# A threshold search by counting: the third count of each round moved from VectorE to ScalarE

## The chip, the cores and the metric

The kernel runs on one core of one Trainium2 chip. Its time is the device time of one execution in microseconds, the median of several runs. The core's engines are named as in the profile: PE is TensorE (PEld its weight loads), ACT is ScalarE, DVE is VectorE, POOL is GpSimd and SP is SyncE, which here only issues DMAs. Each engine runs its own instructions in order.

## The reference

One inference step of a decoder layer, for a prompt of 1024 tokens and for a sample of 8 sequences with 4 new tokens each over a paged past of 8192. Sparse attention and retention run side by side:

```python
hp = _rmsnorm(xp, g_pre[i])
qa, ka, va, qi, ki, wi, ga, qb, kb, vb, gb = _project(hp, w_in[i], pos_p)
oa = _dsa_prompt(qa, ka, va, qi, ki, wi, rel_bias)          # top-256 keys by an indexer, then attention
ob, sp = _retention(qb, kb, vb, zeros)                       # 8 heads, chunks of 128
xp = _merge(xp, oa, ob, ga, gb, p_prompt[i], w_out[i], g_post[i], w_ple_up[i], w_ple_gate[i])
...
oa = _dsa_sample(qa, ka, va, qi, ki, wi, cache_k[i], cache_v[i], cache_kidx[i], page_table, rel_bias)
ob, ss = _retention(qb, kb, vb, state_ret[i])
```

The change lies in the selection of the sample's keys. In the reference this is

```python
score = jnp.einsum('bqh,bqhs->bqs', wi, jax.nn.relu(s))     # 32 queries, 8196 keys each
score = jnp.where(valid, score, -jnp.inf)
top_val, top_idx = lax.top_k(score, topk)                   # topk = 256
```

The kernel does not sort. For each of the 32 queries it looks for the threshold that 256 scores reach, and then selects by comparison.

## The kernel before, in words

The order of the work is: norms, projections and index scores (the signs of the search start at 317.6 us, the first projection of head pair 0 at 297); retention over four pairs of heads, `hp` 0 to 3; attention of the prompt, with the sample's attention threaded through it; output projection and gate.

The threshold search of the sample, `bisect_sample`, runs beside the retention. The 32 queries' scores lie on 128 partitions: partition 32·i + q holds a quarter i of query q's keys, in 2048 + 32 columns (`NX`). `u16` holds the upper 16 bits of each score, turned so that they order as unsigned numbers. `search` finds in eight rounds the 16-bit threshold of each query, two bits a round: with a step `s` that is divided by four each round, three thresholds are tried, and the number of scores at or above each is compared with 256. A count is had in one of two ways. `signs` lets ScalarE compute Sign(x + bias) over the 2080 columns and sum the signs in the same instruction. The other way is VectorE's compare with a threshold and a sum (L974), here in three pieces of 704, 688 and 688 columns, each followed by a tiny instruction (L978) that turns a count into a sum of signs. Before the change the outer two thresholds of a round are counted on ScalarE and the middle one, `mid`, on VectorE.

The three sums stand in `sgn`; `totals` adds the four partitions of a query by a small matmul (L940), whose result every partition gets. ScalarE then takes the sign of each total against the wanted number and sums the three signs into `up` (L984), by which VectorE moves `mid` (L985) and ScalarE sets the next biases (L956) from `pre`, which GpSimd had moved by 0.75 `s` beforehand (L961).

After the rounds the tail of the selection follows (L997 to L1085): one more count, the lower 16 bits, the exact threshold, and a mask that goes out by DMA (L1085). `sample_select` starts from it (L1326) and is threaded through the retention of the later head pairs.

Beside it, each head pair of the retention projects 8 blocks of 128 tokens to q and k (`pqk`) and to v and gate (`pvg`), 24 matmuls a block (L287 to L289), into three PSUM banks of tag "b". The q and k blocks are rotated by VectorE (L1116 to L1118) and GpSimd (L1120, L1121). The v and gate blocks are read by ScalarE (L1129, L1131). `chunk_mm` transposes q and k, ScalarE copies them (qkT, L1142), VectorE masks the scores (L1148) and adds up the state (L1610), and ScalarE copies the chunk's result (acc, L1618). ScalarE also rounds the weights of the next projection (L196).

The order of the instructions is set when the kernel is built: the framework lists all of them, and puts them in order per engine by priority, by what is ready, and by its own estimate of durations. `bisect_sample` is a generator that `steps` advances by one piece per block of head pair 0, from the third block on, at high priority; `sample_select` is advanced in head pairs 1 to 3.

Of the kernel before, what the change touches and what calls it, by code (L numbers as in the profile page):

```python
# [11 lines left out]
F32 = mybir.dt.float32  # L12
F32R = mybir.dt.float32r
BF16 = mybir.dt.bfloat16
# [3 lines left out]
ALU = mybir.AluOpType  # L18
# [113 lines left out]
def tile_step(ctx: ExitStack, tc: tile.TileContext, I, O):  # L132
    nc = tc.nc

    def pool(name, bufs=1, **kw):
        return tc.tile_pool(name=name, bufs=bufs, reuse_waits="tile", **kw)
# [18 lines left out]
    def bank(name, tag="b"):  # L155
        if tag in kept.get("tags", ()):
            return kept["pool"].tile([128, 512], F32, tag="s", bufs=1, name=name)
        return psum["pool"].tile([128, 512], F32, tag=tag, bufs=psum["bufs"][tag], name=name)
# [351 lines left out]
    with pool("ix", side="right") as ix:  # L510
# [131 lines left out]
        for i in range(4):  # L642
            nc.vector.tensor_scalar(place[:, i * 256:i * 256 + 256], C("slots"), i * 256.0, -1.0e-36,
                                    op0=ALU.add, op1=ALU.mult)
# [250 lines left out]
    NX = 2048 + NS  # L895
    stk = ExitStack()

    def bisect_sample():


        V = nc.vector
        ss_ = stk.enter_context(pool("sst", side="right"))
# [18 lines left out]
        sgn = ss_.tile([128, 4], F32R, name="sgn")  # L921
# [10 lines left out]
        def signs(src, bias, j):  # L932

            with nc.allow_low_precision(reason="whole numbers up to NX"):
                nc.scalar.activation(jk, src, AF.Sign, bias=bias, accum_out=sgn[:, j:j + 1])

        def totals():

            t = bank("stot", "t")[:, 0:4]
            nc.tensor.matmul(t, groupr, sgn, start=True, stop=True)  # L940
            return t

        def search(src, k, mid):


            s = float(1 << 14)
            b = None
            V.memset(mid, 2 * s - 0.5)
            pre = ss_.tile([128, 4], F32, tag="pre", bufs=2, name="pre")
            for j in range(2):  # L950
                nc.gpsimd.memset(pre[:, j:j + 1], 0.5 - (3 - 2 * j) * s)
            for r in range(8):
                if r:
                    b = pre[:, 2:4]
                    for j in range(2):
                        nc.scalar.activation(b[:, j:j + 1], up, AF.Identity, bias=pre[:, j:j + 1], scale=-2.0 * s)  # L956
                        signs(src, b[:, j:j + 1], j)
                    if r < 7:
                        pre = ss_.tile([128, 4], F32, tag="pre", bufs=2, name="pre")
                        for j in range(2):  # L960
                            nc.gpsimd.tensor_scalar(pre[:, j:j + 1], b[:, j:j + 1], 0.75 * s * (1 - 2 * j), None,  # L961
                                                    op0=ALU.add)
                else:
                    for j in range(2):
                        signs(src, pre[:, j:j + 1], j)
                    p0, pre = pre, ss_.tile([128, 4], F32, tag="pre", bufs=2, name="pre")
                    for j in range(2):
                        nc.gpsimd.tensor_scalar(pre[:, j:j + 1], p0[:, j:j + 1], 0.75 * s * (1 - 2 * j), None,
                                                op0=ALU.add)
                c2 = ss_.tile([128, 5], F32, tag="c2", bufs=2, name="c2")  # L970
                part = -float(NX)
                for j, c, w in ((0, 0, 704), (1, 704, 688), (2, 1392, 688)):
                    jv = ss_.tile([128, 704], BF16, tag="jv", bufs=1, name="jv")
                    V.tensor_scalar(jv[:, :w], src[:, c:c + w], mid, None, op0=ALU.is_ge, op1=ALU.add,  # L974
                                    accum_out=c2[:, j:j + 1])
                    to = c2[:, 3 + j:4 + j] if j < 2 else sgn[:, 2:3]
                    with nc.allow_low_precision(reason="whole numbers up to NX"):
                        V.tensor_scalar(to, c2[:, j:j + 1], 2.0, part, op0=ALU.mult, op1=ALU.add)  # L978
                    part = to
                t = totals()  # L980

                st = ss_.tile([128, 4], F32, tag="st4", bufs=2, name="st4")
                up = st[:, 3:4]
                nc.scalar.activation(st[:, 0:3], t[:, 0:3], AF.Sign, bias=k, accum_out=up)  # L984
                V.scalar_tensor_tensor(mid, up, s / 2, mid, op0=ALU.mult, op1=ALU.add)  # L985
                s /= 4
                yield

        hi16 = Xt.bitcast(U16).rearrange("p (n two) -> p n two", two=2)
        V.memset(sgn.bitcast(F32), 0.0)  # L990
# [3 lines left out]
        V.scalar_tensor_tensor(u16, lw, 1 << 15, hi16[:, :, 1], op0=ALU.bitwise_xor, op1=ALU.bitwise_xor)  # L994
        yield
        yield from search(u16, k1, tu)
        V.tensor_scalar(bias, tu, -1.0, -0.5, op0=ALU.mult, op1=ALU.add)  # L997
        signs(u16, bias, 0)
# [87 lines left out]
        yield  # L1086

    bss = bisect_sample()


# [43 lines left out]
    def chunk_mm(qk, vv, tb, rows, mask_ap, hp):  # L1134

        r = bank("ret", "c")
        nc.tensor.transpose(r[:, 0:rows], qk[:rows, 0:128], ident[:rows, :rows])
        nc.tensor.transpose(r[:, 128:128 + rows], qk[:rows, 128:256], ident[:rows, :rows])
        qkT = rt.tile([128, 256], F32, tag="qkT", bufs=2, name="qkT")
        rv = r[:, :256].rearrange("p (a r) -> p a r", a=2)[:, :, :rows]  # L1140
        qv = qkT.rearrange("p (a r) -> p a r", a=2)[:, :, :rows]
        nc.scalar.copy(qv, rv)  # L1142
        e = second[:, (tb % 4) * 128:(tb % 4) * 128 + 128]
        sm = rt.tile([128, 2, 128], F32, tag="sm", bufs=2, name="sm")
        for j, sc in enumerate((r[:rows, 256:256 + rows], e[:rows, :rows])):
            js = slice(j * 64, j * 64 + 64)
            nc.tensor.matmul(sc, qkT[js, 128:128 + rows], qkT[js, 0:rows], start=True, stop=True)
            nc.vector.tensor_tensor(sm[:rows, j, :rows], sc, mask_ap, op=ALU.mult)  # L1148
        return r, qkT, sm
# [416 lines left out]
    for hp in range(4):  # L1566
# [27 lines left out]
        for tb in range(8):  # L1594
# [8 lines left out]
            r, qkT, sm = chunk_mm(qk, vv, tb, 128, tri, hp)  # L1603
# [112 lines left out]
    for qb in range(8):  # L1716
# [7 lines left out]
        w = min(n, 256)  # L1724
# [3 lines left out]
        for kv in range(2):  # L1728
# [5 lines left out]
            for i4 in range(4):  # L1734
# [5 lines left out]
                for c in range(0, n, 512):  # L1740
                    wc = min(512, n - c)
                    s = bank("sa")
# [3 lines left out]
                    for x0, x1, add in ((c, cut, mask[:, OFF.get(qb, 0) + c:OFF.get(qb, 0) + cut]),  # L1746
                                        (cut, c + wc, near[:, h - 4 * kv, cut - n + 256:c + wc - n + 256])):
                        if x1 > x0:
                            latest[0] = nc.vector.tensor_tensor_reduce(  # L1749
                                L[:, x0:x1], s[:, x0 - c:x1 - c], add, 1.0, least,  # L1750
                                op0=ALU.add, op1=ALU.min, accum_out=mn[:, i:i + 1]).ins
                            least, i = mn[:, i:i + 1], i + 1
                behind[0] = nc.scalar.activation(L[:, :n], L[:, :n], AF.Exp, bias=least, scale=-1.0,  # L1753
                                                 accum_out=sm[:, i4:i4 + 1])
# [22 lines left out]
            for i4 in range(4):  # L1777
                o, c2 = i4 // 2, i4 % 2
# [227 lines left out]
```

## Time and profile before

| | |
|---|---|
| Time, median of 3 runs | 1019.05 us (1011.37 to 1019.05) |
| The profiled execution | 1009.07 us, span 1007.0 us |
| Mean granted TensorE clock | 0.969 |
| PE, DVE, ACT, POOL busy in the span | 945.4, 664.2, 453.5, 338.8 us |
| The eight rounds of the search | 317.6 to 384.3 us from the start of the span |
| The sample's selection after it, L1326 | 435.3 us |

Times in rows of the profile are microseconds from the start of the span, unless they are marked as a mean or a median in ns. In a row of a group, `xN | a, b | c <-X c` says that N instructions were busy for a us together, b ns each on average, and that the engine sat idle for c us just before them, most of it until X was done. In a row of waits, `A <- B: t, n, m` says that A waited for B t us in all, n times, the longest m us. In a row of stretches, each engine's busy us stand with the number of its instructions, and then the granted clock, the DMA share and GB/s. In a row of the timeline, a start and a duration come first, and idle time before the instruction stands in brackets.

### The profile page before, as it was taken

Reading aid. Unit: us, or ns where it says so; the run is one execution under the profiler, and the core shown is the slowest. Engines: PE = TensorE matmul, PEld = TensorE weight load, DVE = VectorE, ACT = ScalarE, POOL = GpSimd, SP = SyncE. Lnnn points to the kernel's source line nnn. Section 1 sums busy time; section 2 is a strip of 40 time slices with the busy share of each in tenths; the row PEclk is TensorE's granted clock in tenths of the full one; section 3 lists DMA queues with packets and bytes.
Section 4 is the critical chain, followed back from the end, with each engine's and each line's share of the span. In section 5 each row is a group of like instructions: output and inputs, shape, how many; then the busy total and the mean of one; then the engine's idle time right before and its main releaser. Section 6 shows DMA issues by size and latency. Waiting matters only on the chain.

```text
span 1007.0 us, 18956 instructions
## 1 busy us (share of the span) xinstructions
PE 945.4 (94%) x6983; PEld 798.3 (79%) x6983; DVE 664.2 (66%) x1936; ACT 453.5 (45%) x1005; POOL 338.8 (34%) x444
## 2 busy tenths in 40 slices
PE   4999995989999999998899988999999999999998
PEld 3989993557678988988898866566567999999998
DVE  6747667879946669889679558777754323953332
ACT  5645555345324877224422537465554434432210
POOL 4205215112406326247325226454323322233300
PEclk8999998899999999999899968999999999999999
DMA  8323234567534112032013554533221312422211
GB/s 277 100 73 102 100 111 119 188 206 255 182 104 102 41 43 69 20 91 67 24 43 102 135 162 138 163 105 97 63 79 55 112 53 84 143 86 90 86 39 37
DMA packets 102127, 104.36 MB, mean 104 GB/s; under 512 B 22002, under 2 KB 92210, under 8 KB 99602
## 3 DMA queue, kind: packets, MB, share of 16 engines
q1 hardware_dynamic: 96274, 76.93, 25.8%
q0 software_dynamic: 5760, 26.22, 8.4%
q8 instruction: 55, 0.90, 0.4%
q14 instruction: 38, 0.31, 0.1%
HBM read 80.36 MB, written 22.76 MB: 102 GB/s over the span
## 4 chain that ended last, share of the span: by engine, by line
PE 63%; DVE 14%; DMA 9%; issue 8%; POOL 3%; ACT 2%; SPq 1%; DVEq 0%; POOLq 0%; ACTq 0%
PE pb L277 5%; PE pb L278 4%; PE pb L279 4%; PE ob L1772 3%; PE ptp L1764 3%; PE pg L287 3%; PE pg L289 3%; PE pg L288 3%; PE po L287 3%; PE po L288 3%; PE po L289 3%; PE pox L877 2%; DMA kx<-in_cache_kidx,kidx 2%; PE pvg L287 2%; PE pvg L288 2%
## 5 line engine op out<-in xcount | busy, mean ns | idle before, releaser
L1277 POOL DMA_INDIRECT kvs<-in_cache_kv,idx x64 | 64.2, 1004 | 59.0 <-ACT pT L1769 32.0
L287 PE MATMUL pvg<-whi_vgb,xh 128*128 128x256 f32 x256 | 77.0, 301 | 2.5 <-DVE rp L1118 2.5
L288 PE MATMUL pvg<-wlo_vgb,xh 128*128 128x256 f32 x256 | 75.8, 296 | 0.8 <-POOL wlo_vgb L197 0.8
L287 PE MATMUL pqk<-whi_qkb,xh 128*128 128x256 f32 x256 | 73.8, 288 | 1.5 <-DVE rp L1118 1.2
L289 PE MATMUL pvg<-whi_vgb,xl 128*128 128x256 f32 x256 | 74.6, 292 | 0.0
L287 PE MATMUL po<-whi_o,yTh 128*128 128x256 f32 x256 | 73.3, 286 | 0.4 <-DVE yaT L1783 0.4
L288 PE MATMUL pqk<-wlo_qkb,xh 128*128 128x256 f32 x256 | 73.3, 287 | 0.0
L289 PE MATMUL pqk<-whi_qkb,xl 128*128 128x256 f32 x256 | 73.1, 285 | 0.0
L288 PE MATMUL po<-wlo_o,yTh 128*128 128x256 f32 x256 | 72.9, 285 | 0.0
L287 PE MATMUL pg<-whi_g,yTh 128*128 128x256 f32 x256 | 72.7, 284 | 0.0
L289 PE MATMUL po<-whi_o,yTl 128*128 128x256 f32 x256 | 72.6, 284 | 0.0
L289 PE MATMUL pg<-whi_g,yTl 128*128 128x256 f32 x256 | 72.3, 282 | 0.0
L288 PE MATMUL pg<-wlo_g,yTh 128*128 128x256 f32 x256 | 72.2, 282 | 0.0
L197 POOL TENSOR_TENSOR wlo_g<-wraw_g,whi_g 128x256 fp32r<-128x256 f32 x32 | 27.1, 881 | 88.0 <-ACT whi_g L196 87.9
L1961 DVE TENSOR_TENSOR sgm<-pu,sgm 128x256 f32<-128x256 f32 x32 | 13.6, 424 | 64.5 <-PE pu L289 61.2
L1753 ACT ACTIVATE L<-L,mn 128x128 f32<-128x128 f32 (+7 forms) x64 | 49.6, 777 | 14.5 <-DVE mn L1749 14.1
L543 DVE SCALAR_TENSOR_TENSOR score<-r,wi,score 128x384 f32<-128x384 f32 (+5 forms) x42 | 42.6, 1015 | 20.2 <-ACT r L542 18.2
L287 PEld LDWEIGHTS pvg<-whi_vgb,xh 128*128 128x128 f32 x256 | 50.0, 195 | 4.6 <-issue 2.1
L288 PEld LDWEIGHTS pvg<-wlo_vgb,xh 128*128 128x128 f32 x256 | 50.0, 195 | 1.3 <-POOL wlo_vgb L197 1.0
L287 PEld LDWEIGHTS pqk<-whi_qkb,xh 128*128 128x128 f32 x256 | 48.3, 188 | 3.1 <-issue 2.4
L287 PEld LDWEIGHTS po<-whi_o,yTh 128*128 128x128 f32 x256 | 49.0, 191 | 2.2 <-issue 1.6
L289 PEld LDWEIGHTS pvg<-whi_vgb,xl 128*128 128x128 f32 x256 | 50.1, 196 | 0.3
(559 smaller groups left out, 3115.9 us busy)
## 6 DMA issues: line engine op xcount, KB each, us to landing
wraw_qkb<-in_w_in SPq DMA_DIRECT2D x16, 256.0 KB
wraw_vgb<-in_w_in SPq DMA_DIRECT2D x16, 256.0 KB
wraw_o<-in_w_out SPq DMA_DIRECT2D x8, 512.0 KB
qas<-qas_d SPq DMA_DIRECT2D x8, 512.0 KB
xr<-in_x_prompt SPq DMA_DIRECT2D x8, 512.0 KB
wraw_g<-in_w_ple_gate SPq DMA_DIRECT2D x8, 512.0 KB
out_y_prompt<-sgm SPq DMA_DIRECT2D x32, 128.0 KB
qas_d<-qst SPq DMA_DIRECT2D x8, 384.0 KB
```

The source lines that it names most:

```text
L197: nc.gpsimd.tensor_tensor(lo[:, k, :n], raw, hi[:, k, :n].bitcast(F32), op=ALU.subtract)
L277: nc.tensor.matmul(pt[:m, :n], wh, xh[:, k, ts], start=(k == 0), stop=False)
L278: nc.tensor.matmul(pt[:m, :n], wh, xl[:, k, ts], start=False, stop=False)
L279: nc.tensor.matmul(pt[:m, :n], wl, xh[:, k, ts], start=False, stop=(k == KC - 1))
L287: nc.tensor.matmul(pt[:, :n], ah, hi[:, k, :n], start=(k == 0), stop=False)
L288: nc.tensor.matmul(pt[:, :n], ah, lo[:, k, :n], start=False, stop=False)
L289: nc.tensor.matmul(pt[:, :n], al, hi[:, k, :n], start=False, stop=(k == kc - 1))
L543: nc.vector.scalar_tensor_tensor(sc, r[:, :n], wi[:, qb, h:h + 1], sc if h else place[:, :n], op0=ALU.mult, op1=ALU.add)
L1277: return nc.gpsimd.indirect_dma_start(out=dst, out_offset=None, in_=kvflat, in_offset=bass.IndirectOffsetOnAxis(ap=idx, axis=0))
L1753: behind[0] = nc.scalar.activation(L[:, :n], L[:, :n], AF.Exp, bias=least, scale=-1.0, accum_out=sm[:, i4:i4 + 1])
L1764: nc.tensor.transpose(tp[:, i4 * 128:i4 * 128 + 128], P[i4][:, kb * 128:kb * 128 + 128], ident)
L1772: nc.tensor.matmul(ob[64 * o:64 * o + 64, :256], vtok[:, kb, kv * 64:kv * 64 + 64], pT[:, o * 256:o * 256 + 256], start=(kb == 0), stop=(k ...
```

## The change

In all eight rounds, the middle threshold is counted as the other two are: by a third `signs` over the 2080 columns, with a bias of its own. The three pieces of compare-and-sum on VectorE, the instructions that turn counts into sums of signs, and the move of `mid` in each round are gone. The third bias is made as the others are: ScalarE adds -2 `s` times `up` to `pre`, whose third column GpSimd copies on without a shift. `mid` is worked out once, after the last round, from the third bias. `totals` and the decision stay.

```diff
             s = float(1 << 14)
-            b = None
-            V.memset(mid, 2 * s - 0.5)
             pre = ss_.tile([128, 4], F32, tag="pre", bufs=2, name="pre")
-            for j in range(2):
-                nc.gpsimd.memset(pre[:, j:j + 1], 0.5 - (3 - 2 * j) * s)
+            for j, c in enumerate((0.5 - 3 * s, 0.5 - s, 0.5 - 2 * s)):
+                nc.gpsimd.memset(pre[:, j:j + 1], c)
+            b = pre
             for r in range(8):
                 if r:
-                    b = pre[:, 2:4]
-                    for j in range(2):
+                    b = ss_.tile([128, 4], F32, tag="c2", bufs=2, name="c2")
+                for j in range(3):
+                    if r:
                         nc.scalar.activation(b[:, j:j + 1], up, AF.Identity, bias=pre[:, j:j + 1], scale=-2.0 * s)
-                        signs(src, b[:, j:j + 1], j)
...
-                c2 = ss_.tile([128, 5], F32, tag="c2", bufs=2, name="c2")
-                part = -float(NX)
-                for j, c, w in ((0, 0, 704), (1, 704, 688), (2, 1392, 688)):
-                    jv = ss_.tile([128, 704], BF16, tag="jv", bufs=1, name="jv")
-                    V.tensor_scalar(jv[:, :w], src[:, c:c + w], mid, None, op0=ALU.is_ge, op1=ALU.add,
-                                    accum_out=c2[:, j:j + 1])
-                    to = c2[:, 3 + j:4 + j] if j < 2 else sgn[:, 2:3]
-                    with nc.allow_low_precision(reason="whole numbers up to NX"):
-                        V.tensor_scalar(to, c2[:, j:j + 1], 2.0, part, op0=ALU.mult, op1=ALU.add)
-                    part = to
+                    signs(src, b[:, j:j + 1], j)
                 t = totals()
 
                 st = ss_.tile([128, 4], F32, tag="st4", bufs=2, name="st4")
                 up = st[:, 3:4]
                 nc.scalar.activation(st[:, 0:3], t[:, 0:3], AF.Sign, bias=k, accum_out=up)
-                V.scalar_tensor_tensor(mid, up, s / 2, mid, op0=ALU.mult, op1=ALU.add)
-                s /= 4
+                if r < 7:
+                    pre = ss_.tile([128, 4], F32, tag="pre", bufs=2, name="pre")
+                    for j in range(3):
+                        nc.gpsimd.tensor_scalar(pre[:, j:j + 1], b[:, j:j + 1], (0.75 * s, -0.75 * s, 0.0)[j], None,
+                                                op0=ALU.add)
+                    s /= 4
                 yield
+            V.scalar_tensor_tensor(mid, up, s / 2, b[:, 2:3], op0=ALU.mult, op1=ALU.subtract)
```

More of the change, by code (lines that the diff above doesn't have):

```diff
@@ L956, in search @@
                         nc.scalar.activation(b[:, j:j + 1], up, AF.Identity, bias=pre[:, j:j + 1], scale=-2.0 * s)
-                        signs(src, b[:, j:j + 1], j)
[L958 to L969, printed above, removed]
```

## The prediction

> **What bounds the kernel now.** I read the page first, for what carries the span and for the chain that ended last. The profiled execution took 1009.07 us, of which 1007.0 are its span; 2.07 us lie around it.
>
> ```profile
> span 1007.0 us, 18956 instructions
> PE 945.4 (94%) x6983; PEld 798.3 (79%) x6983; DVE 664.2 (66%) x1936; ACT 453.5 (45%) x1005; POOL 338.8 (34%) x444
> ...
> PE 63%; DVE 14%; DMA 9%; issue 8%; POOL 3%; ACT 2%; SPq 1%; DVEq 0%; POOLq 0%; ACTq 0%
> ```
>
> TensorE is busy 94% of the span and holds 63% of the chain; ScalarE holds 2%. But the change works in one stage only, so I asked the trace for the stretch of the eight rounds, from the first sign (317.6) to the last round's decision (384.3). The second row below is that stretch for the signs (L935) alone.
>
> ```profile
> core 0: us, PE busy (x) PEld busy (x) DVE busy (x) ACT busy (x) POOL busy (x), PEclk, DMA share, GB/s
> 317.60:384.30 66.70, 64.89 (x546) 59.23 (x547) 49.85 (x187) 53.61 (x116) 24.43 (x52) 1.00 0.13 34
> 317.60:384.30 66.70, 33.87 (x32) 1.00 0.13 34
> ```
>
> In these 66.70 us TensorE works 64.89, on the retention matmuls of the first two head pairs, at full clock. ScalarE, 45% busy over the span, is busy 53.61 of 66.70 here (80%), VectorE 49.85 (75%). So this stage is TensorE's, with ScalarE the fuller of the two helpers. What TensorE waited for in it, and where the DVE counts stand on the chain (first and last of eight pieces, 7.2 us together), I read next:
>
> ```profile
> POOL pre L961 <- ACT pre L956: 22.2, 4, 8.8
> ...
> PE pqk L287 <- DVE rp L1118: 1.2, 1, 1.2
> ...
> PE stot L940 <- ACT sjk L935: 0.5, 1, 0.5
> PE ret L1616 <- DVE sbd L1612: 0.4, 1, 0.4
> ```
>
> ```profile
> 318.26 0.87 DVE jv L974 x2
> 333.99 0.97 DVE jv L974 x2
> ```
>
> TensorE waited 1.2 us on a rotation, 0.5 on a sign and 0.4 on a state sum. The rotation's wait is over before the first count (the chain has the counts from 318.26 on), so it is not theirs; the state sum stood between two of them. The counts are on the chain until 336, but the runner-up there is TensorE itself, never more than 1.8 us (66.70 - 64.89) behind.
>
> **What goes.** From VectorE, all of the count:
>
> ```profile
> L974 DVE TENSOR_SCALAR_CACHE_REDUCE jv<-su,ssm 128x688 bf16<-128x688 uint16 (+1 forms) x24 | 22.3, 928 | 0.2
> L974 DVE DVE_READ_ACCUMULATOR jv<-su,ssm 128x1 f32 x24 | 2.0, 83 | 0.0
> L978 DVE TENSOR_SCALAR c<-c 128x1 f32<-128x1 f32 x16 | 2.9, 180 | 0.3
> L978 DVE TENSOR_SCALAR sgn<-c 128x1 fp32r<-128x1 f32 x8 | 1.7, 211 | 0.2
> L985 DVE SCALAR_TENSOR_TENSOR ssm<-st,ssm 128x1 f32<-128x1 f32 x7 | 1.5, 217 | 5.1 <-ACT st L984 5.1
> ```
>
> 22.3 + 2.0 + 2.9 + 1.7 + 1.5 = 30.4 us of work, 3.8 per round, less one L985 that stays at the end; VectorE falls from 49.85 to about 20 us of the stretch. What that gives TensorE is bounded above by its idle 1.8 us, and below by nothing. I take the 0.4 of the one wait that stood behind counts. By the Trainium skill, Perfetto Trace Analysis, section Identifying the Most-Contended Engine, matmul busy time is a poor measure and the busy share of weight loads the better one: by that row TensorE has 66.70 - 59.23 = 7.5 us free, and this gain could reach 7.5.
>
> **What comes.** On ScalarE, a third sign in each round and a third bias in seven of them:
>
> ```profile
> L935 ACT ACTIVATE sjk<-su,pre 128x2080 bf16<-128x2080 uint16 x16 | 32.4, 2024 | 2.2 <-issue 2.0
> L935 ACT ACTIVATION_READ_ACCUMULATOR sjk<-su,pre 128x1 fp32r x16 | 3.0, 188 | 0.0
> L956 ACT ACTIVATE pre<-st,pre 128x1 f32<-128x1 f32 x14 | 3.3, 285 | 0.4
> L984 ACT ACTIVATE st<-stot,ssm 128x3 f32<-128x3 f32 x8 | 2.1, 265 | 4.0 <-PE stot L940 4.0
> L984 ACT ACTIVATION_READ_ACCUMULATOR st<-stot,ssm 128x1 f32 x8 | 1.6, 198 | 0.0
> ```
>
> A sign with its readout takes 33.87 / 16 = 2.12 us (they overlap a little), a bias 3.3 / 14 = 0.24. Eight signs are 17.0 us, seven biases 1.7: 18.6 us more. 53.61 + 18.6 = 72.2 us of ScalarE work for a stretch of 66.70: **ScalarE no longer fits**, by 5.5 us. That is the core of this change. GpSimd gets one memset and six more shifts of `pre` (L961), on an engine that waited 22.2 us in this stretch for just these biases: hidden, and without that cover 0.2 to 0.5 us a round.
>
> The length of a round follows from the first one, in which ScalarE does almost nothing else, and from the last decision:
>
> ```profile
> 317.61 2.03 ACT L935 ACTIVATE sjk<-su,pre 128x2080 bf16<-128x2080 uint16 x1 [2.02 <-issue]
> 319.76 2.03 ACT L935 ACTIVATE sjk<-su,pre 128x2080 bf16<-128x2080 uint16 x1
> 322.60 0.26 ACT L984 ACTIVATE st<-stot,ssm 128x3 f32<-128x3 f32 x1 [0.71 <-PE stot L940]
> 322.99 0.48 ACT L956 ACTIVATE pre<-st,pre 128x1 f32<-128x1 f32 x2
> 323.37 2.01 ACT L935 ACTIVATE sjk<-su,pre 128x2080 bf16<-128x2080 uint16 x1
> ...
> 383.96 0.26 ACT L984 ACTIVATE st<-stot,ssm 128x3 f32<-128x3 f32 x1 [0.43 <-PE stot L940]
> ```
>
> Decision to first sign 0.77 us, sign to sign 2.15, last sign to the next decision 2.84 (with the matmul of the totals between). With two signs a round needs 0.77 + 2.15 + 2.84 = 5.76 us of ScalarE's own chain; measured are (383.96 - 322.60) / 7 = 8.77. With three it needs 0.77 + 0.19 + 2 x 2.15 + 2.84 = 8.10. Now the ends: with nothing else on ScalarE the search ends at 317.6 + 7.1 + 7 x 8.10 = 381; with today's 3.0 us of other things per round kept, at 402. Between them: the other ScalarE work in the stretch is 53.61 - 33.87 - 3.3 - 3.7 = 12.7 us, and if all of it stands in line, 394. I take 394, **10 us later than now**, because the engine is then simply full.
>
> **Who waits behind the third sign.** ScalarE runs in order, and TensorE needs its small copies: v and the gate (L1129, L1131) free the three projection banks, qkT (L1142) and acc (L1618) carry the chunk. Other work does slip in between two signs (a qkT copy ahead of a round's second one, rows below), and a projection tile takes TensorE 3.45 us from one first matmul to the next (the two rows after):
>
> ```profile
> 352.37 0.38 ACT L1142 COPY qkT<-ret 128x256 f32<-128x256 f32 x1
> 352.62 2.06 ACT L935 ACTIVATE sjk<-su,pre 128x2080 bf16<-128x2080 uint16 x1
> ```
>
> ```profile
> 325.74 0.39 PE L287 MATMUL pvg<-whi_vgb,xh 128*128 128x256 f32 x1
> 329.19 0.39 PE L287 MATMUL pvg<-whi_vgb,xh 128*128 128x256 f32 x1
> ```
>
> Three banks are 3 x 3.45 = 10.3 us of run-ahead; three signs back to back are 6.4. So most of it is covered, and where the cover is gone TensorE pays the sign, 2.1 us a round. No row shows ScalarE full. Bounds: nothing (the search alone comes late), or all eight third signs, 17.0. The overflow of 5.5 is the nearest row; I take 4 of it, as some falls on the search.
>
> **What comes late.** The search's result goes through the rest of the selection (about 387 to 430) to the sample's selection at L1326; SyncE waits for the last step of it.
>
> ```profile
> 390.00:400.00 10.00, 8.64 (x76) 7.21 (x75) 9.94 (x19) 7.42 (x19) 7.73 (x13) 1.00 0.35 88
> 400.00:410.00 10.00, 9.73 (x71) 8.68 (x70) 9.79 (x28) 3.47 (x12) 7.61 (x12) 1.00 0.51 124
> L1326 DVE TENSOR_TENSOR eq<-X,tq x1: 2293/2293/2293, 435.3 to 435.3; 128x2048 bf16<-128x2048 f32 x1
> SPq L1085 <- DVE sjk L1084: 12.9, 1, 12.9
> ```
>
> From 390 to 410 VectorE is full, and TensorE loses 1.36 + 0.27 = 1.6 us: the tail of the search meets the first head pair's norm and state. Ten microseconds later it meets other work. Best case those 1.6 us come back; worst case the whole 10 pass on, since SyncE, GpSimd and VectorE stand in order behind the tail. I take 0: the two shifts are of one cause and of opposite sign.
>
> **Sum.** -0.4 + 4 + 0 = +3.6 us: 1009.07 becomes 1012.7. The runs shown lie at 1011.37 to 1019.05, median 1019.05, so the profiled execution was 10 us quicker than the median; on the median's scale the forecast is 1019.05 + 3.6, some 1022. One per cent, 10 us, is about what a measurement of this kernel can tell from no change.
>
> **Rivals.**
> - *ScalarE becomes the bound (slower).* Place: the copies of L1129, L1131, L1142, L1618 behind the signs, 318 to 395. It decides once the delay exceeds the 10.3 us of the three banks, that is, once copies wait through a whole round. Price 17.0: 1036. For it: 72.2 us of work in 66.7. Against it: work slips in between signs today. Chance 0.24. [...]
> - *VectorE's share of the chain comes back (faster).* The 7.2 us of counts go from the chain and 1.6 more after 390: -8.8, 1010. For it: VectorE's 14% of the chain (141 us) and its full rows. Against: TensorE idle 1.8 us only, and the 4 us of late copies. Chance 0.20, of which 0.10 past one per cent: that needs over 1 us more of VectorE's other shares of the chain.
> - *The late tail stands in the way (slower).* The queues behind L1085 and L1326 carry the next weights and rotations; 10 us pass on to TensorE: 1031. It decides when the tail is later than the slack of those loads. Against: SyncE already waits 12.9 us there at no visible cost. Chance 0.12, half of it past one per cent.
> - That the change does not do what it says I leave at nothing: the new lines leave VectorE no instruction within a round.
>
> **How the numbers follow.** The forecast has the remaining 0.44, its own range 1016 to 1030 (from -1.8 - 1.6 to the overflow of 5.5 with half of the tail's 10). Faster 0.10; slower 0.24 + 0.06 = 0.30; within one per cent 0.44 + 0.10 + 0.06 = 0.60. The range goes from 1003, the quickest run shown (1011.37) less 8.8, to the first rival's 1036.
>
> **What would show it.** Right: ScalarE over 90% busy between 318 and 390, rounds of 9 to 10 us, the last decision some 10 us later, VectorE near 20 us in the stretch, and TensorE's waits on ScalarE a few microseconds. Wrong: rounds of 8 us or less (then nothing comes late and the gain stands alone), or waits of pvg and ret matmuls on L1129, L1142 and L1618 of over 10 us (the first rival), or TensorE idle after 430 where it was not (the third).

## The result, and the profile after

The changed kernel took 1004.15 us (median of 11 runs, 1002.51 to 1009.04) beside 1013.16 for the kernel before on the same chip: ratio 0.9909, interval [0.9887, 0.9931]. Two repeats gave 0.9922 [0.9896, 0.9947] and 0.9895 [0.9865, 0.9925]. I had forecast 3.6 us more; it is about 9 us less.

The profiled execution took 1003.3 us. From its page, the span, the busy times and the chain by engine:

```profile
span 1001.5 us, 18899 instructions
PE 938.3 (94%) x6983; PEld 793.6 (79%) x6983; DVE 636.5 (64%) x1856; ACT 464.3 (46%) x1024; POOL 327.8 (33%) x452
...
PE 70%; DMA 10%; DVE 10%; issue 4%; ACT 3%; POOL 2%; SPq 2%; another core or an unknown queue 0%; ACTq 0%; DVEq 0%; POOLq 0%
```

VectorE lost 27.7 us of work, ScalarE gained 10.8 (less than the third signs and biases take, in part because it has 12 instructions `ACT_TABLE_LOAD` of 1.28 us instead of 16), and TensorE holds 70% of the chain instead of 63%. The search itself became much longer. The stretch from the first round's decision to the last, then ScalarE's largest groups in it, and what TensorE waited for from 318 to 425:

```profile
324.80:417.10 92.30, 91.00 (x768) 84.00 (x763) 39.02 (x164) 80.06 (x177) 34.17 (x73) 1.00 0.18 47
```
```profile
L935 ACT ACTIVATE sjk<-su,c 128x2080 bf16<-128x2080 uint16 x21 | 42.5, 2026 | 0.2
...
L1169 ACT ACTIVATE acc<-acc,gz,gy 128x64 f32<-128x64 f32 (+1 forms) x14 | 4.9, 428 | 1.3 <-DVE gz L1165 1.3
L956 ACT ACTIVATE c<-st,pre 128x1 f32<-128x1 f32 x21 | 4.7, 292 | 0.2
L196 ACT CAST whi_qkb<-wraw_qkb 128x1024 fp32r<-128x1024 f32 x4 | 4.2, 1048 | 1.6 <-DMA wraw_qkb<-in_w_in 1.6
...
L935 ACT ACTIVATION_READ_ACCUMULATOR sjk<-su,c 128x1 fp32r x21 | 4.0, 190 | 0.0
...
L962 ACT ACTIVATE st<-stot,ssm 128x3 f32<-128x3 f32 x8 | 2.1, 262 | 4.8 <-PE stot L940 4.8
L962 ACT ACTIVATION_READ_ACCUMULATOR st<-stot,ssm 128x1 f32 x8 | 1.6, 195 | 0.0
```
```profile
PE pqk L287 <- DVE rp L1101: 1.2, 1, 1.2
PE pvg L287 <- ACT sg L1114: 1.1, 1, 1.1
PE ret L1588 <- ACT vv L1112: 0.2, 1, 0.2
```

Seven rounds take 92.3 us, 13.2 each instead of 8.8, and the last decision falls at 417 instead of 384: 33 us later. Signs and their readouts, which overlap a little, are 44.5 of ScalarE's 80.06 us, and the biases (L956) and decisions (L962) 8.4; the other 27.2 are the retention's work, into which the longer search runs (above all v, L1112, the gated norm L1169 and the weights' casts L196 of the next pair). But TensorE waited for ScalarE only 1.3 us in all of this.

VectorE is no longer full from 390 to 410 us, and TensorE idles almost as long there as before (1.04 + 0.24 us instead of 1.36 + 0.27):

```profile
390.00:400.00 10.00, 8.96 (x79) 7.56 (x78) 5.09 (x20) 9.66 (x21) 7.59 (x18) 1.00 0.83 213
400.00:410.00 10.00, 9.76 (x81) 9.51 (x81) 2.87 (x12) 9.92 (x27) 3.87 (x6) 1.00 0.01 2
```

Idle time is not the whole of it, though: TensorE has 160 matmuls in these 20 us instead of 147, though not all are of one size. So I compared the same work, from head pair 1's first value matmul to the end of head pair 2's q and k, first before, then after the change:

```profile
391.90:463.50 71.60, 69.00 (x567) 62.11 (x566) 63.46 (x185) 24.70 (x73) 33.10 (x45) 1.00 0.26 63
```
```profile
390.30:459.10 68.80, 67.00 (x572) 61.55 (x573) 47.49 (x177) 37.22 (x91) 24.01 (x44) 1.00 0.19 48
```

It took 2.8 us less: 71.6 us in both profiles of before, and 68.8, 69.1 and 70.8 in the three of the change (the last with 1.7 us lost to the clock). This is where the tail of the search ran before. The work ahead of it, beside most of the rounds, took as long as before (94.4 us from head pair 0's start in both). The larger part of the gain lies in neither place. To find it I took, in every profile, the stretch from the first q/k matmul of head pair 0 to the sample's first matmul of the output projection (the prompt's begin some 17 us sooner), with the same TensorE instructions in all kernels, but for a few at the rounded ends. First the kernel before and its second profile, then the change, its third profile, and the fastest kernel of this study (all counts of VectorE kept as dead work, below):

```profile
297.50:786.70 489.20, 465.24 (x3684) 379.14 (x3677) 356.38 (x1242) 246.02 (x592) 205.15 (x276) 0.97 0.31 85
```
```profile
296.50:788.50 492.00, 468.40 (x3688) 382.19 (x3681) 356.45 (x1242) 245.76 (x592) 203.73 (x276) 0.95 0.31 84
```
```profile
295.90:782.00 486.10, 460.71 (x3684) 376.22 (x3676) 327.65 (x1162) 257.14 (x611) 193.53 (x283) 0.96 0.31 85
```
```profile
294.90:772.80 477.90, 455.22 (x3684) 372.41 (x3676) 327.49 (x1162) 256.70 (x611) 194.66 (x283) 0.98 0.32 87
```
```profile
295.90:764.10 468.20, 453.08 (x3688) 371.71 (x3684) 342.85 (x1234) 256.89 (x611) 194.04 (x283) 0.98 0.33 88
```

Such a row splits into three: TensorE idle (length less PE busy), lost to the clock (length times one less the granted clock, here from the unrounded clock), and the rest, TensorE's work at full clock. The last column but one tells when the selection's eight largest values (MAX8, the middle of the tail) were taken. Ratios are against the kernel before on the same chip.

| kernel | ratio | length | idle | clock | rest | MAX8 at | signs a round |
|---|---|---|---|---|---|---|---|
| before | | 489.2 | 24.0 | 17.1 | 448.2 | 398 | 2 |
| before, again | 1.0005 | 492.0 | 23.6 | 22.2 | 446.2 | 398 | 2 |
| one small copy | 0.9986 | 486.2 | 23.7 | 13.7 | 448.8 | 397 | 2 |
| three small copies | 1.0023 | 493.0 | 24.5 | 20.5 | 448.1 | 412 | 2 |
| before, low parts on VectorE | 0.9921 | 480.6 | 21.9 | 10.2 | 448.4 | 398 | 2 |
| before, casts held | 0.9980 | 490.9 | 25.3 | 15.4 | 450.2 | 398 | 2 |
| tail held sooner | 0.9982 | 489.5 | 27.2 | 15.4 | 447.0 | 419 | 2 |
| tail held | 0.9949 | 482.3 | 22.2 | 13.7 | 446.4 | 435 | 2 |
| third sign added | 0.9982 | 486.4 | 20.6 | 22.2 | 443.6 | 426 | 3 |
| change | 0.9909 | 486.1 | 25.4 | 17.1 | 443.6 | 425 | 3 |
| change, again | 0.9922 | 482.7 | 23.9 | 13.7 | 445.1 | 429 | 3 |
| change, third | 0.9895 | 477.9 | 22.7 | 10.2 | 445.0 | 424 | 3 |
| change, tail held | 0.9887 | 482.2 | 18.8 | 18.8 | 444.6 | 429 | 3 |
| change, low parts on VectorE | 0.9920 | 484.3 | 22.3 | 18.8 | 443.3 | 428 | 3 |
| change, casts held | 0.9917 | 484.3 | 26.1 | 13.7 | 444.5 | 425 | 3 |
| change, narrow dead counts | 0.9880 | 482.2 | 22.7 | 17.1 | 442.5 | 427 | 3 |
| change, counts kept dead | 0.9836 | 474.5 | 19.1 | 10.2 | 445.2 | 423 | 3 |
| the same, again | 0.9792 | 468.2 | 15.1 | 8.5 | 444.6 | 421 | 3 |

The change's own 8.4 us (490.6 on average in the two profiles of before, 482.2 in its three) are: idle time none (23.8 and 24.0), the clock 6 (19.7 and 13.7), the rest 2.6 (447.2 and 444.6). Single profiles scatter by several microseconds in the clock column; over all runs the mean granted clock says 3 us, 2 to 5 by set (the clock lost 26.6, 28.3, 25.7 and 27.3 us of the span of before, and 24.3, 22.9, 23.9 and 24.4 of the change or a kernel with its order, in the same four sets). The clock column can also overstate a loss: ahead of the stretch, the first profile of before lost 13.7 us to the clock and the second 6.8, and they took 297.5 and 296.5 us.

### The profile page after: what moved, and what is told of

Read it like the earlier page. It is cut to its first block, busy times and chain, and to the rows that moved or that the text cites. A ratio compares the mean times of both kernels' runs of the same rounds, so it can differ in the third digit from the quotient of the medians.

```text
span 1001.5 us, 18899 instructions
## 1 busy us (share of the span) xinstructions
PE 938.3 (94%) x6983; PEld 793.6 (79%) x6983; DVE 636.5 (64%) x1856; ACT 464.3 (46%) x1024; POOL 327.8 (33%) x452
## 4 chain that ended last, share of the span: by engine, by line
PE 70%; DMA 10%; DVE 10%; issue 4%; ACT 3%; POOL 2%; SPq 2%; another core or an unknown queue 0%; ACTq 0%; DVEq 0%; POOLq 0%
PE pb L277 5%; PE pb L278 4%; PE pb L279 4%; PE ob L1755 4%; PE ptp L1747 3%; PE pg L287 3%; PE pg L289 3%; PE pg L288 3%; PE po L287 3%; PE po L288 3%; PE po L289 3%; PE pvg L287 2%; PE pvg L289 2%; PE pvg L288 2%; PE pox L877 2%
## 5 line engine op out<-in xcount | busy, mean ns | idle before, releaser
L1103 POOL TENSOR_TENSOR qk<-rp,rp 128x128 f32<-128x128 f32 (+1 forms) x36 | 17.4, 482 | 104.5 <-DVE rp L1100 69.0
L287 PEld LDWEIGHTS pg<-whi_g,yTh 128*128 128x128 f32 x256 | 48.7, 190 | 1.6 <-issue 1.2
```

Source lines behind the costliest of these rows:

```text
L287: nc.tensor.matmul(pt[:, :n], ah, hi[:, k, :n], start=(k == 0), stop=False)
```

## The experiments

Theory V: the gain is VectorE's 30 us of freed work. Theory L: it is the tail that comes 33 us later. Theory O: it is the order of the instructions, which the build finds anew for every edit. Two more came up on the way: C, collisions of the tail's long VectorE passes with GpSimd and with the state sums; and H, the half clock at the end of the retention.

**The change once more.**

> The changed kernel, on the same chip as the others: all theories expect a ratio near 0.991.

Measured 0.9922 [0.9896, 0.9947].

**Third sign added, VectorE's counts left as they were.** It goes to an unused column.

```diff
 # kernel before, in each round
+signs(src, (b if r else p0)[:, 1:2], 3)
```

> The kernel before, with a third sign per round on ScalarE whose sum goes into the unused fourth column of sgn: VectorE counts as before, ScalarE is as full and the search as late as in the changed kernel. Theory V (the gain is VectorE's freed 30 us): no gain, ratio 0.998 to 1.005. Theory L (the gain is that the search's tail comes some 30 us later, away from where VectorE was full): about 0.991. Theory O (only the order of instructions that the build happened to find): anything within 1%, not tied to the others.

0.9982 [0.9961, 1.0002], with the last decision at 417.2, as late as the change's. That is what Theory V had said, and Theory L missed. But in its profile the rest is the change's (443.6) and idle time is less (20.6 us); what took the gain back is the clock (22.2), with 30.7 us of half clock at the end of the retention that began within a wait of 5.4 us for a state sum.

**Two signs only.** The middle count is left out.

```diff
 # changed kernel
-    signs(src, b[:, j:j + 1], j)
+    if j < 2:
+        signs(src, b[:, j:j + 1], j)
-V.scalar_tensor_tensor(bias, k2, 8.0, ...)
+V.scalar_tensor_tensor(bias, k2, 8.0e9, ...)
```

> The changed kernel without its third sign: the middle count is left out (so thresholds are not the right ones, and the repair loop is kept from starting by an out-of-reach bound). VectorE is freed as in the changed kernel, but ScalarE has 17 us less and the search ends early, near 375. Theory V: 0.991 or lower. Theory L: 0.997 to 1.003, since the tail meets the same full stretch. Theory O: anything within 1%.

1.0172 [1.0136, 1.0208]. The wrong thresholds change what the attention gathers (its stretch took 200 us instead of 187), so this one compares only with its twin below.

**Tail held, rounds untouched.** From L997 on the tail is queued on VectorE behind the state sum of head pair 1's chunk 3, and the sample's selection starts only after it.

```diff
 # kernel before, head pair 1, after chunk 3
+with tc.issue_after(summed.ins), tc.high_priority():
+    step(bss)                    # and the rest of bss behind it
```

> The kernel before with its rounds untouched; only the search's tail (from L997) is queued on VectorE behind the state sum of the second head pair's fourth chunk, so that it starts near 420 instead of 387, and the sample's selection follows it. Theory V: 0.998 to 1.002. Theory L: about 0.991. Theory O: anything within 1%.

0.9949 [0.9927, 0.9971], MAX8 at 435. The hold gives half a per cent with all of VectorE's counts in place; that is half of what Theory L said. Whether by lateness or by the other order that it brings about, this run does not tell.

**Counts kept as dead work in the changed kernel.**

```diff
 # changed kernel, in each round
+for j, c, w in ((0, 0, 704), (1, 704, 688), (2, 1392, 688)):
+    V.tensor_scalar(jv[:, :w], src[:, c:c + w], b[:, 2:3], ..., accum_out=cd[:, j:j + 1])
+    ...                          # L978's sums, the last into sgn[:, 3:4]
```

> The changed kernel, with VectorE's three counting pieces of every round put back as dead work: they count against the middle threshold and write an unused column of sgn, and nothing reads it. ScalarE has its three signs and the tail of the selection stays as late as in the changed kernel (the eight largest at about 425 us instead of 398), but VectorE is as full in the rounds as before. It is the mirror of the run that only added the third sign (ratio 0.998). Theory V (the gain is VectorE's 30 us of freed work): most of the gain goes, ratio 0.996 to 1.000. Theory L (the gain is the late tail): the gain stays, ratio 0.991 to 0.994, as the changed kernel. Theory O (luck of the order that the build finds): anything, with no relation to either pair.

0.9836 [0.9806, 0.9867]: faster than the change, with VectorE's work given back. **Theory V falls**, and neither L nor O had said so; this is the fastest kernel here. Nor can any account by load alone hold: this kernel and the one with the third sign added do three signs and all of VectorE's counts in every round, and lie 1.5 per cent apart (1.9 in the repeat below). What differs is which count the decision reads, and the order.

**Change and tail held**: the change with the edit of "tail held".

> The changed kernel, and its tail held back in VectorE's queue behind the state sum of head pair 1's chunk 3, as the run that held the tail of the kernel before (ratio 0.995). The eight largest come at about 435 us instead of 425. If lateness and VectorE's relief are two separate gains that add up, and lateness pays on from 425 to 435: ratio 0.988 to 0.991. If lateness is spent by 425: as the changed kernel, 0.991 to 0.994. If the hold takes the place of the relief (both give the same idle time back): 0.994 to 0.996.

0.9887 [0.9855, 0.9918], within the change's own repeats. MAX8 came at 429, hardly later than without the hold, so it could not tell whether lateness pays on.

**Two signs, counts dead**: "two signs only" with the dead counts. The middle count stays out of the decision.

> The run with two signs only (ratio 1.017), with VectorE's counting kept as dead work whose result nothing reads; the middle count is left out of the decision as there, so thresholds and selection are the same wrong ones in both and the two runs compare with each other. The tail comes early in both (the eight largest at about 397 us); only VectorE's load in the rounds differs, by 30 us. Theory V: it is 3 to 6 us slower than the run with two signs only, ratio 1.020 to 1.023. Theory L: the same as that run, 1.016 to 1.019; the counts ran beside other work.

1.0109 [1.0067, 1.0150], against 1.0172 for its twin. With the tail early as well, the counts do not make it slower: V falls a second time. The ratio lies below Theory L's range too.

**Tail held sooner**, behind chunk 1.

```diff
-if hp == 1 and tb == 3:
+if hp == 1 and tb == 1:
```

> The kernel before with its tail held as in the earlier hold, but behind the state sum of head pair 1's chunk 1 instead of chunk 3: the eight largest at about 415 us (398 before, 435 with the longer hold, which gave 0.995). Rounds and counts untouched. Theory L with a collision in the stretch where VectorE is full (390 to 410 us): some of the gain already, ratio 0.996 to 0.998. The prediction's term (ten microseconds of lateness are worth nothing): 0.999 to 1.001. If lateness is not what paid there but the order of the queue after chunk 3: 1.000 or above.

0.9982 [0.9962, 1.0002], MAX8 at 419. With twenty microseconds of lateness went 0 to 0.4%; with the 37 of the longer hold 0.3 to 0.7.

**Where the change loses again.** Its profile showed a collision in head pair 2 that the kernel before does not have. VectorE and GpSimd around it, and what TensorE waited for from 459 to 502:

```profile
476.88 7.15 DVE L1321 TENSOR_TENSOR_SCAN cx<-eq,cx 128x1056 f32<-128x1056 bf16 x1
484.06 0.42 DVE L301 TENSOR_TENSOR sh_vg<-pvg,sh_vg 32x256 f32<-32x256 f32 x1
484.51 0.47 DVE L1595 COPY sbd<-ret 64x64 f32<-64x64 f32 x2
```
```profile
476.54 2.81 POOL L197 TENSOR_TENSOR wlo_qkb<-wraw_qkb,whi_qkb 128x256 fp32r<-128x256 f32 x4
479.32 0.45 POOL L1174 TENSOR_TENSOR acc<-acc,sgs 32x128 f32<-32x128 f32 x1
479.74 4.81 POOL L197 TENSOR_TENSOR wlo_qkb<-wraw_qkb,whi_qkb 128x256 fp32r<-128x256 f32 x4
```
```profile
PE ret L1599 <- DVE sbd L1595: 5.7, 1, 5.7
PE ret L1588 <- DVE sm L1131: 1.0, 1, 1.0
```

A scan of the sample's selection took 7.15 us while GpSimd made eight low parts of weights back to back; the state sum (L1595) stood behind it, and TensorE waited 5.7 us. In the kernel with the dead counts (second run) the same scan, with the same run of eight under way, takes 2.40 us, and it is GpSimd's run that gets longer (8.48 us, where eight of 0.73 make 5.8). TensorE's longest wait on that state sum is 1.0. A collision like the change's doesn't decide the time alone: the kernel before with its tail held has it too (a scan of 7.14 us, a wait of 5.7) and gained half a per cent. The kernel with the dead counts:

```profile
473.45 2.40 DVE L1331 TENSOR_TENSOR_SCAN cx<-eq,cx 128x1056 f32<-128x1056 bf16 x1
```
```profile
472.04 8.48 POOL L197 TENSOR_TENSOR wlo_qkb<-wraw_qkb,whi_qkb 128x256 fp32r<-128x256 f32 x8 [1.72 <-ACT whi_qkb L196]
```
```profile
PE ret L1609 <- DVE sbd L1605: 1.0, 1, 1.0
```

**Low parts on VectorE**, in the changed kernel and as a control in the kernel before:

```diff
-nc.gpsimd.tensor_tensor(lo[:, k, :n], raw, ...)
+eng = nc.vector if name == "qkb3" else nc.gpsimd
+eng.tensor_tensor(lo[:, k, :n], raw, ...)
```

> The changed kernel, with the eight subtractions that make the low parts of head pair 3's q/k weights on VectorE instead of GpSimd. In the changed kernel's profile the second scan of the sample's selection (L1321) took 7.15 us instead of 2.4, while GpSimd ran eight of these subtractions back to back; the state sum behind it on VectorE came late, TensorE waited 5.7 us, and a stretch at half clock followed. Theory C (collisions of the tail's long VectorE passes with GpSimd and with the state sums decide the time): the scan takes 2.4 us, head pair 2's stretch of values and gates shrinks from 42.8 to 37 or 38 us, and the ratio falls from 0.991 to 0.984 to 0.988. Theory O (the order that the build finds, without one cause to name): anything between 0.983 and 0.998, with the loss at other places. Theory V (VectorE's free time was the gain): slower by the 3 us of work given back, 0.993 to 0.996.

> The same edit on the kernel before, as the control: there the scans run at 442 and 446 us, when GpSimd makes other weights, and took 2.35 and 2.83 us, so there is nothing to win for them. Theory C: ratio 0.997 to 1.003. Theory O: anything from 0.984 to 1.010.

In the changed kernel with this edit the scan took 2.40 us, the 5.7 us wait became 2.2 at most, and head pair 2's stretch of values and gates fell from 42.8 to 39.0 us, as C said. But the ratio is 0.992 [0.9891, 0.9949], no better than the change's: a new wait came up in head pair 3, with 30.7 us of half clock behind it:

```profile
PE psl L1366 <- DVE lo__5036 L1374: 5.0, 1, 5.0
```

The control missed: 0.9921 [0.9891, 0.9952], where Theory C had 0.997 to 1.003, by an edit that touches nothing of the search. Its stretch in head pair 2 fell from 43.5 to 38.8 us.

**Both compared on one chip.**

> The run with VectorE's counts kept as dead work beside all three signs, once more, beside the changed kernel on the same chip. If its 0.984 was its own: 0.982 to 0.987 again, and its profile again without the long scan. If it was the chip or the run: 0.990 to 0.994.

> The changed kernel itself, as the comparison for the two kernels built from it in this set: 0.990 to 0.993, with a scan of 7.1 us and a wait of 5.7 us in its profile again.

0.9792 [0.9759, 0.9826] and 0.9895 [0.9865, 0.9925]: the dead counts win again, both with their own scan (2.40 and 7.13 us).

**Order alone.** The position of every instruction can be compared between two builds. The change moves some 1820 of TensorE's 6238 and 910 of VectorE's. Four runs on that:

```diff
 # kernel before, in each round, once or three times
+V.tensor_copy(nul[:, j:j + 1], up)
 # narrow dead counts: as the dead counts, with
-((0, 0, 704), (1, 704, 688), (2, 1392, 688))
+((0, 0, 8), (1, 704, 8), (2, 1392, 8))
```

> The kernel before, unchanged: a second profile of it and the spread that no edit makes. Ratio 0.998 to 1.002. If its losses belong to its order of instructions, the profile shows them at the same places: head pair 2's and 3's stretches of values and gates at about 43 and 57 us, the waits of 1.9, 1.4 and 2.3 us in the first of them. If they are of one execution: elsewhere, or gone.

> The kernel before, with one copy of a single column (128x1) on VectorE added in every round of the search, which nothing reads: some 1.5 us of VectorE's work in all. Counting positions in each engine's list of instructions, the build moves about 300 of TensorE's 6238 instructions and 112 of VectorE's 1986. Theory O (the order that the build finds decides more than the loads): another ratio than 1, anywhere from 0.985 to 1.01. Theories V and L (freed work, late tail): 1.000 to 1.002, for neither is touched.

> As the run with one small copy, with three of them in every round, some 4 us of VectorE's work in all. The build moves about 1950 of TensorE's instructions and 680 of VectorE's, as many as the change under study (1820 and 910). Theory O: anywhere from 0.98 to 1.01, and 0.990 as likely as the change's own. Theories V and L: 1.000 to 1.004, slightly slower for the work added.

> The run with VectorE's counts kept as dead work beside the three signs (ratios 0.984 and 0.979), with every piece cut to 8 columns: the same instructions and dependences, a tenth of the work. The order of TensorE is that of the changed kernel but for 6 instructions. Theory O: as the changed kernel, 0.989 to 0.993, with the scan of 7.1 us again, since the wide counts helped only by another order. If the counting instructions themselves helped (as spacing between the signs): 0.979 to 0.985.

1.0005 [0.9979, 1.0031], 0.9986 [0.9965, 1.0008], 1.0023 [1.0001, 1.0045] and 0.9880 [0.9842, 0.9919]. The losses of before keep their places in its second profile (43.3 and 58.0 us for the two stretches). Shuffling alone, even of 1950 instructions, gave no gain in two tries. The narrow counts, with the change's order, behave as the change (a scan of 7.14 us too). So it is not the counting instructions as such that help; the wide ones bring another order and more load, and no run here tells these two apart.

**The half clock.** In the kernel before, ScalarE's group and TensorE's wait ahead of the long half clock, with the stretches around it:

```profile
581.75 1.99 ACT L196 CAST whi_o<-wraw_o 128x1024 fp32r<-128x1024 f32 x2 [1.94 <-PE pvg L289]
583.65 0.36 ACT L1142 COPY qkT<-ret 128x256 f32<-128x256 f32 x1
```
```profile
PE ret L1147 <- ACT qkT L1142: 1.4, 2, 1.3
```
```profile
578.60:582.00 3.40, 3.40 (x30) 3.36 (x30) 1.74 (x6) 1.10 (x5) 0.00 (x0) 1.00 0.14 41
582.00:585.70 3.70, 2.44 (x19) 1.73 (x18) 1.23 (x5) 3.23 (x6) 2.77 (x5) 1.00 0.67 198
585.70:589.00 3.30, 3.30 (x13) 2.73 (x14) 1.46 (x7) 0.59 (x3) 2.73 (x5) 0.50 1.09 353
```

TensorE pauses 1.26 us for a copy that stands behind two casts, and from 585.7 on its clock is halved (the second profile of before has the same). That is 14 us ahead of the attention (13 in the second profile of before); in the three profiles of the change the long half clock begins 1 to 4 us ahead of it. Both kernels with the casts held:

```diff
-wt = [load_w("o0", [(w_out[:, 0:256], 256)])]
+with tc.issue_after(copied[0]):  # the last qkT copy
+    wt = [load_w("o0", [(w_out[:, 0:256], 256)])]
```

> The kernel before, with the two casts of the first output weights (L196, 1.0 us each on ScalarE) held in ScalarE's queue behind the last qkT copy of the retention. In both profiles of the kernel before they stand ahead of a qkT copy at 582 to 584 us, TensorE pauses 1.26 us for it, and a stretch at half clock of 24 and 27 us begins 3 us later, with the last chunks of head pair 3 still to come. Everything up to there keeps its order; search and tail are untouched. Theory H (most of the change's gain is that this stretch at half clock begins later and is shorter): head pair 3's stretch of values and gates falls from 57 or 58 us to 52 to 54, the half clock to 10 to 20 us, ratio 0.993 to 0.997. If the pause has nothing to do with it: 0.999 to 1.001 and the half clock as long as before. If the late weights cost more than the pause: above 1.001.

> The same edit on the changed kernel, as the control: there the retention's end has no pause behind these casts, and its half clock begins only as the attention starts. Theory H: as the changed kernel itself, 0.988 to 0.993. If holding the casts helps for another reason: 0.984 to 0.987.

0.9980 [0.9959, 1.0001] and 0.9917 [0.9890, 0.9944]; the first is short of Theory H's 0.993 to 0.997. The kernel before, then the same with the casts held: head pair 3's values and gates, and the attention.

```profile
543.00:600.10 57.10, 52.69 (x376) 45.74 (x375) 36.20 (x148) 24.54 (x71) 18.37 (x29) 0.84 0.60 165
600.10:786.70 186.60, 178.90 (x1362) 120.20 (x1361) 126.85 (x462) 106.16 (x243) 81.23 (x81) 0.97 0.35 99
```
```profile
542.90:595.10 52.20, 47.81 (x375) 41.90 (x374) 36.27 (x148) 24.44 (x71) 16.04 (x26) 0.93 0.66 178
595.10:788.10 193.00, 184.42 (x1366) 122.00 (x1367) 128.67 (x462) 106.91 (x243) 83.93 (x85) 0.96 0.33 96
```

The stretch lost its 5 us as H said (57.1 to 52.2, the clock 0.84 to 0.93), and the attention took 6.4 longer; the long half clock began at 591.7 instead of 585.7. But the pause by itself does not start it. The kernel with one small copy has the same casts and the same pause, at 582.4 us, and its clock stays full; its long half clock begins at 591.3:

```profile
PE ret L1149 <- ACT qkT L1144: 1.5, 2, 1.3
```
```profile
581.10:584.50 3.40, 2.14 (x19) 1.71 (x18) 1.51 (x4) 3.03 (x5) 2.00 (x3) 1.00 0.53 149
584.50:587.90 3.40, 3.28 (x21) 2.49 (x20) 1.62 (x7) 1.72 (x6) 3.40 (x6) 1.00 1.08 343
```

So the pause's part in the half clock is not shown, and taking it away saved at most 0.4%.

**What is settled, and what is open.** Shown: VectorE's relief is not needed for the gain, for two kernels with the counts put back were no slower than their twins without them (the third sign added, which has the work of the faster of these two, was slower than the change); and ScalarE's third pass does not cost TensorE a visible wait. Not shown is that lateness of the tail is a cause: the longer hold gained half a per cent, but the three small copies, with MAX8 14 us later, gained nothing, and the third sign added, 28 us later, at most 0.4%. In the table, all ten profiles with three signs have a rest of 442.5 to 445.2 us and all eight with two have 446.2 to 450.2: some 3 us that go with the third sign, by way of no single group that I could name. Some 2 us of them lie in the stretch from head pair 1's values to head pair 2's q and k (67.00 instead of 69.00 above). The five profiles put the other 6 us down to half clock, which scatters between executions of one kernel; all runs together put 3 there, and then some 3 of the 9 have no place. Why the change gets less half clock is open. And 0.8% came from an edit beside the search, so a good part of any such difference may be where the order happens to put the collisions; that is argued from these runs, not shown.

## Why the prediction was wrong, point by point

- **What bounds the kernel** held: TensorE is the bound in the rounds (91.00 of 92.30 us busy), and little could be won there from VectorE. The term of -0.4 for its relief is as good as the runs can tell; no run paid for VectorE's load.
- **"Who waits behind the third sign" was the step that failed.** It charged 4 of ScalarE's 5.5 us of overflow to TensorE. TensorE waited 1.3 us on ScalarE, against 0.5 before, and its work beside most of the rounds took 94.4 us both before and after. The argument in the same paragraph, that three banks (10.3 us) cover three signs (6.4), was right and should have set the term to nothing. The first rival fell with it.
- **"What comes"**, on which that step stands, had the work right and its effect wrong. The 18.6 us were right in size, and ScalarE did not fit, but the overflow went wholly into the search: rounds of 13.2 us, not 9 to 10, and the end at 417, 33 us later, past even the bound of 402. I had ended the sum at the other work of the old stretch (12.7 us); a longer search meets more of it (27.2 us by the same working) and, since ScalarE keeps order, its waits too (4.8 us for the totals, 3.1 for weights). ScalarE was 85% busy from 318 to 390, not over 90, and VectorE had 27.4 us in a stretch as long as the old one, not 20.
- **"What comes late" and what the sum left out.** Without the +4 the sum would still say -0.4, not -9. The term of 0 was two shifts of opposite sign. The loss side, queues behind L1085 and L1326, never showed; that was the third rival (whose 1031 does not follow from its 10 us either, which make 1029 on the median's scale). On the gain side at most 1.6 us were seen, as idle time; 2.8 came back around that place, most of it while TensorE counts as busy. The holds changed the time by -0.5% [-0.73, -0.29] at 37 us of lateness and -0.2% at 20, but they change the order as well.
- **The second rival** named the right size (-8.8 us) by luck: VectorE's 7.2 us on the chain were not what came back, for with the counts kept the kernel is faster still.
- **Missing from the sum** was the clock. The half-clock stretches here are multiples of 3.4 us, and the longest, at the end of the retention, took 24 and 27 us before and 10 to 17 in the change. Of the 9 us gained, 2 to 6 are of this kind, far from the edit; what sets them off stays open. The Trainium skill, TensorE: Matmul & The Clock Gate, section What's actually happening, makes the clock depend on TensorE's recent activity in windows of 3.4 us.

## What to carry to other kernels

When work is moved to an engine that seems to have no room, ask first whether the thing that gets longer has slack: here a search could run 33 us later at no cost, and the cover argument (banks of run-ahead against one pass) was worth more than adding up busy time. Before a one-per-cent gain is put down to the work removed, put that work back as dead work: if the gain stays or grows, it was something else. One such build is not enough, though: here two kernels with the same work in every round lay 1.5 per cent apart. Judge an edit of this size over the whole stretch that it can reorder, split into idle time, clock and rest, not in the stage that it touches.

## What the runs showed of the hardware

- A VectorE scan of 1056 columns took 7.13 to 7.15 us in six profiles (the change three times, the change with narrow counts and with casts held, and the kernel before with its tail held) and 2.33 to 3.17 us otherwise. In the change it came 0.3 us into the first of eight GpSimd subtractions of 0.7 us each, and it seems to have waited for seven of them; the last one then took 2.77 us. Why the same scan went ahead after the first subtraction in the kernel with the dead counts is open. The Trainium skill, SBUF — State Buffer, section SBUF: two separate sides, has a port pair that VectorE and GpSimd take turns at, held for a whole instruction; by that rule the scan would lose one subtraction, 0.73 us, and here it lost 4.8.
- The clock was halved after a stretch of 3.7 us in which TensorE was still busy 2.44 us (582.0 to 585.7), and it was not halved in another kernel after 3.4 us with 2.14 busy (581.1 to 584.5). The half clock then lasted 24 and 27 us in the two profiles of before, and 10 to 17 in the change's, though TensorE was busy all of the first 3.3 us of it (585.7 to 589.0). The Trainium skill, TensorE: Matmul & The Clock Gate, section What's actually happening, has the clock halved after at least one idle window of some 3.4 us; here the stretch ahead of it was not idle.
